# A ring of six weight blocks refilled one block at a time, and the heads' outputs transposed one step later, in a two-layer encoder trunk

## The chip, the cores and the metric

The kernel runs on one core of one Trainium2 chip. The time is the device time of one execution in microseconds (us). Before the change three runs gave 1183.42, 1184.66 and 1185.49 us, so the median is 1184.66 us. One further execution was taken with the hardware profiler, and every row of the profile below comes from that one.

## The reference

The kernel computes two layers over a sequence of 512 tokens of width 1024. Layer 0 mixes tokens by differential attention with six heads, and layer 1 by chunked gated linear attention (GLA). Each layer runs, beside its mixer, an attention of four heads into 256 memory tokens, sends all heads' outputs through one output projection, and ends with a gated MLP of inner width 2816 with a causal convolution. The part that the change touches most is the differential attention:

```python
lam = exp(sum(lv[0]*lv[1])) - exp(sum(lv[2]*lv[3])) + lam_init
logits = einsum('bhmqd,bhmkd->bhmqk', qb, k) + bias[rel]
p = softmax(where(visible, logits, -inf))
w = p[:, :, 0] - lam * p[:, :, 1]
o = einsum('bhqk,bhkv->bhqv', w, v)
o = rms_norm(o, out_norm_g) * (1.0 - lam_init)
```

Everything is float32. All weight products keep near float32 precision: each operand is split into a rounded high part and a low rest, and a product is the sum of three matmuls (high by high, high by low, low by high).

## The kernel before

**Weights.** Every weight matrix is cut into blocks of up to 128 x 1024 values, which lie in the order of their use in one packed input, wpack. A block is loaded by SyncE (SP) into one of three `raw` buffers (`load_raw`). ScalarE (ACT) then casts it to its high part `whi` (L203), and VectorE (DVE) subtracts to get the low part `wlo` (L206). whi and wlo each have a ring of five buffers (`WB = 5`), so the cast of a block waits for the last matmul that reads the block five places earlier. Blocks are grouped in pieces: a piece holds the weights of one gemm or one part of a projection, and has up to four blocks. `weights(key)` is called by the first unit of a gemm, and emits the loads, casts and subtractions of all blocks up to the end of the piece after it, in one go.

**Order on the engines.** TensorE (PE) runs its instructions in the order in which the program emits them. On the other engines the tile framework's scheduler orders the instructions that the program emits, with their waits. ACT and DVE each carry out their list in its order: an instruction that waits holds up all that stand behind it. Where the text speaks of the order after the change, it means the list of instructions that the changed program hands to an engine, which is known without a run.

**Fillers.** Projections that aren't urgent stand in a queue of units (`Filler`), each one pass of two k-tiles (six matmuls of 128 x 512). `F.fill(us)` takes units from the queue for about that many microseconds, so that PE has work while ACT and DVE work on the softmax.

**Layer 0.** A loop over steps t from 0 to 20 is written out as a software pipeline. A head has three steps. In step t the program does, in this order: `logits(t)` (matmuls L622 into banks `lg`, then DVE L627 for bias and minimum, and ACT L630 for exp), `values(t-2)` (L660 into a bank `sm`; at each third step the head's norm: squares on ACT L666, then the normed output `o` on DVE L670), `F.fill`, `turn(t-1)` (four transposes L172 into a bank `tp`, copied to SBUF by ACT L648), memory-attention work (`ma`), `F.fill` again, at t = 5, 6, 11, 12 `prepare` of a later head (transposes of `qs` and `ks`, copied with a gain by ACT L589 to qT and kT), and, at each third step from t = 5, `finish(t//3 - 1)`: four transposes of a head's `o` into a `tp` bank, then the split into xsh (ACT L240) and xsl (DVE L241), which the output projection reads much later. At t = 4 and 10 `norms` does the query and key norms of the next pair of heads (squares on ACT L310). There are two `tp` banks used in turn by all transposes, so a group of transposes waits until the group two before it has been copied out. The second memory projection of layer 0, kv of layer 1's memory, is evacuated by ACT L473 and L474.

**The rest.** The GLA layer, the output projections and the MLPs stream their weights through the same ring, with matmuls at L257 to L259 (weights moving) and L274 to L276 (weights stationary). The constants `C` (identity, masks, two unused triangles, ones) are loaded in the first microseconds, with the gate weights `gw` that the GLA layer uses.

Of the kernel before, what the change touches and what calls it, by code (L numbers as in the profile page):

```python
# [11 lines left out]
F32 = mybir.dt.float32  # L12
F32R = mybir.dt.float32r
I32 = mybir.dt.int32
# [10 lines left out]
MEM = 256  # L25
# [4 lines left out]
WTILE = 1024  # L30
HALVES = (6, 5)
XS = 36
WB = 5
STEPS, FILL = (11, 18), (3.7, 1.64, 1.5)

TOGETHER = ((2, 0), (1,), (3,))
# [95 lines left out]
def trunk(ctx, tc, head_d, x_t, mem_t, wpack, cols_a_d, cols_d, conv_d, gate_d, rel_bias, diff_lambda, consts, onehot, out):  # L132
# [26 lines left out]
    def blk(b, w=128):  # L159
        return slice(w * b, w * b + w)  # L160


    C = perm.tile([128, 768], F32, name="C")
    ident, U, BEU = C[:, 0:128], C[:, 128:256], C[:, 256:384]
    MP, MF = C[:, 384:512].bitcast(I32), C[:, 512:640].bitcast(I32)
    ones = C[:, 640:768]
    eps = perm.tile([128, 1], F32, name="eps")
    V.memset(eps, EPS)

# [38 lines left out]
    def raw_tile():  # L208
        return wp.tile([128, WTILE], F32, name="raw", tag="raw", bufs=3)

    def load_raw(raw, n):
        nc.sync.dma_start(raw[:, :n], wpack[at[0], :, :n])
        at[0] += 1
        return raw

    def make_piece(raws=None, between=None):
        parts = []
        for i, (_, _, kk, _, w) in enumerate(blocks[len(made)]):
            n = len(kk)
            raw = load_raw(raw_tile(), n * w) if raws is None else raws[i]  # L220
            hi, lo = (wp.tile([128, WTILE], F32R, name=t, tag=t, bufs=WB) for t in ("whi", "wlo"))
            if between is not None and i == 3:
                between()
            split_weights(slice(0, n * w), raw, hi, lo, len(made) == 2)
            parts += [(hi[:, blk(j, w)], lo[:, blk(j, w)]) for j in range(n)]
        made.append(parts)

    used = [0]

    def weights(key):  # L230
        i = used[0]
        assert plan[i][0] == key, (plan[i][0], key)
        while len(made) < min(i + 2, len(plan)):
            make_piece()
        used[0] += 1
        parts, made[i] = made[i], None
        return parts

    def split(hi, lo, src, gain):
        A.activation(hi, src, AF.Copy, scale=gain)  # L240
# [5 lines left out]
    def gemm(sh, sl, nb, key, w, evac, hook=None):  # L246
        got, open_ = [], {}

        def unit(b, k0, k1):
            if not got:  # L250
                got.extend(weights(key))
            if k0 == 0:
                open_[b] = bank("mm")[:, :w]
            p = open_[b]
            for k in range(k0, k1):
                hi, lo = got[k]
                mm(p, sh[k][:, blk(b)], hi, start=k == 0, stop=False)  # L257
                mm(p, sh[k][:, blk(b)], lo, start=False, stop=False)  # L258
                mm(p, sl[k][:, blk(b)], hi, start=False, stop=k == KT - 1)  # L259
            if k1 == KT:  # L260
                if hook is not None and b == 0:
                    hook()
                evac(b, open_.pop(b))
        for b in range(nb):
            for k in range(0, KT, 2):
                F.add(6 * w / 2370.0, lambda b=b, k=k: unit(b, k, k + 2))
# [16 lines left out]
    cols_a = perm.tile([128, 32], F32, name="cols_a")  # L283
    cols = perm.tile([128, 26], F32, name="cols")
    cv = [perm.tile([128, 4, NJ], F32, name=f"cv{l}") for l in range(2)]
    gw = perm.tile([96, 384], F32, name="gw")
    nlam = perm.tile([128, 1], F32, name="nlam")
    kmT = [perm.tile([128, 2, MEM], F32, name=f"kmT{l}") for l in range(2)]
    vm = [perm.tile([128, 2, MEM], F32, name=f"vm{l}") for l in range(2)]
    r_x = perm.tile([128, 3, 4], F32, name="r_x")  # L290
    r_mem = perm.tile([128, 2], F32, name="r_mem")

# [30 lines left out]
            V.tensor_copy(bs[c.start // 512], p[:6, :n])  # L323

    def lam(lv, lp):
        l2 = small("l2")[:, :2]
        lv4 = lv.rearrange("p (a c b) -> p a c b", a=2, c=2)
        V.tensor_mul(lp, lv4[:, :, 0], lv4[:, :, 1])
        V.reduce_sum(l2, lp, axis=AX.X)
        A.activation(l2, l2, AF.Exp)  # L330
        V.scalar_tensor_tensor(nlam, l2[:, 1:2], -LAM_INIT, l2[:, 0:1], op0=ALU.add, op1=ALU.subtract)
# [29 lines left out]
    with tc.tile_pool(name="ini", bufs=1) as ip, tc.manual_schedule(engines={E.Activation, E.DVE, E.Pool, E.SP}):  # L361
# [21 lines left out]
            load(raws[k // 2][:, blk(k % 2, S)], wpack[k // 2, :, blk(k % 2, S)])  # L383
        load(cols_a, cols_a_d)
        at[0] = 4
        load(C[:, 640:768], consts[:, 640:768])
        load(rb, rel_bias)
        load(oh, onehot)
        second = [load_raw(raw_tile(), WTILE) for _ in range(3)]
# [1 line left out]
        load(lv, diff_lambda[0].rearrange("a b -> (a b)").partition_broadcast(128))  # L391
        parts, acc, split_w = [], [None], [None]
        made.append(parts)

        def operands(k):
            if k % 2 == 0:
# [17 lines left out]
        for k in range(KT):  # L414
            if k + 1 < KT:
                operands(k + 1)
            if k == 0:
                second.append(load_raw(raws[0], WTILE))
            if k == 4:
                bias_rows(rb, oh, bs)  # L420
            if k == KT - 2:
                make_piece(second, lambda: token_rsqrt("lg", acc[0], NB, r_x[:, 0]))
                weights(("qk", 0))
                small_vectors()
                for c in range(2):
                    load(bias_d[:, 512 * c:min(512 * c + 512, 640)], bs[c])
            hi, lo = parts[k]
            terms = (xh[k], hi), (xh[k], lo), (xl[k], hi)
            full, left, right = slice(0, S), blk(0, S // 2), blk(1, S // 2)
            todo = [(b, i, full) for b in range(NB) for i in range(3)]  # L430
            if k == 0:
                todo = [(0, 0, left), (1, 0, left), (0, 0, right), (1, 0, right)] + sorted(
                    [u for u in todo if u[:2] not in ((0, 0), (1, 0))], key=lambda u: u[1])
            for b, i, t in todo:
                xp, w = terms[i]
                mm(first[b][:, t], xp[:, blk(b)], w[:, t], start=k == 0 and i == 0 and t is not right,
                   stop=k == KT - 1 and i == 2)

    load(C[:, 0:640], consts[:, 0:640])
    for i in range(4):  # L440
        load(memT[i], mem_t[i])
    for l in range(2):
        load(cv[l].rearrange("p a b -> p (a b)"), conv_d[l])
    G.memset(gw, 0.0)
    for b in range(3):
        load(gw[32 * b:32 * b + 17], gate_d)

    mem_acc = [None]

# [104 lines left out]
    def diff_layer(pool, mix, acc):  # L554
        r = r_x[:, 0]
        qm = pool.tile([128, NB, MEM], F32, name="qm", bufs=1)

        v0 = pool.tile([128, NB, 256], F32, name="v0", bufs=1)
        v12 = pool.tile([128, NB, 512], F32, name="v12", bufs=1)
        vs = [v0, v12[:, :, 0:256], v12[:, :, 256:512]]  # L560
# [135 lines left out]
        for t in range(21):  # L696
            if t == 0:
                project_qk(1)
                ops0, keys0 = mem_kv(0)
                gemm(xh, xl, NB, ("v", 1), 512, lambda b, p: A.activation(  # L700
                    v12[:, b], p, AF.Copy, scale=r[:, b:b + 1]))
                F.mark("v1")
                project_qk(2)
            if t == 2:
                ops0()
                ma.norm()
            if t == 10:
                ops1, keys1 = mem_kv(1)
                ops1()
            if t == 16:  # L710
                keys1()
            if t == 12:
                load_x(x_t)
                out_proj(0, mix, 0, None)
            if t == 18:
                rest = out_proj(0, mix, 1, acc, 5)
            f = FILL[bisect(STEPS, t)]
            m = t - M0
            if t < 18:
                logits(t)  # L720
            if 0 <= t - 2 < 18:
                values(t - 2)
            if t == 6:
                keys0("tp")
            F.fill(f)
            if t in (4, 10):
                norms((t + 2) // 6, 0)
                norms((t + 2) // 6, 1)
            if 0 <= t - 1 < 18:
                turn(t - 1)  # L730
            if 1 <= m < 5:
                ma.turn(2 * m - 2)
            if m in (3, 5):
                ma.values(m // 2 - 1)
            if 0 <= m < 4:
                ma.logits(m)
            if t == 20:
                F.flush()
            F.fill(f)
            if 1 <= m < 5:  # L740
                ma.turn(2 * m - 1)
            if t == 3:
                ma.queries()
            if t in (5, 6, 11, 12):
                prepare(2 * ((t + 1) // 6) + (t + 1) % 6)
            if t % 3 == 2 and t >= 5:
                finish(t // 3 - 1)
        rest()
        F.flush()

# [1 line left out]
    def gla_layer(pool, mix, acc):  # L752
# [6 lines left out]
        gl = pool.tile([128, NB, 16], F32, name="gl", bufs=1)  # L759
        gl3, gw3 = split_tiles()  # L760
        gl3, gw3 = gl3[:96], gw3[:96, :384]
        rq, rh = small("rq"), small("rh")

        def scales():
            token_rsqrt("sm", acc[0], NB, r_x[:, 2], True)
# [39 lines left out]

        G.memset(gl3.bitcast(F32), 1.0)
        G.memset(gl3[32:64].bitcast(F32), 0.0)
        A.copy(gw3, gw)
        V.tensor_sub(gw3[64:96], gw[64:96], gw3[64:96].bitcast(F32))
        F.fill(1.0)  # L810
# [313 lines left out]
def _constants():  # L1124
# [2 lines left out]
    i = np.arange(128)  # L1127
    same = (i[:, None] // 64) == (i[None, :] // 64)
    le = i[:, None] <= i[None, :]
    c = np.zeros((128, 768), np.float32)  # L1130
    c[:, 0:128] = np.eye(128)
    c[:, 128:256] = same & le
    c[:, 256:384] = same & ~le
    c[:, 384:512] = same & le
    c[:, 512:640] = same & ~le
    c[:, 640:768] = 1.0

    rel = np.arange(640) - 511
    n = np.abs(rel)
# [57 lines left out]
```

## Time and profile before

| what | value |
|---|---|
| median of three runs | 1184.66 us |
| the profiled execution, its own time | 1182.33 us |
| span of its instructions | 1180.5 us |
| so around the span | 1.8 us |
| PE | busy 99% of the span |
| PE weight loads | busy 82% |
| DVE | busy 64% |
| ACT | busy 46% |
| DMA | 117.81 MB at a mean of 100 GB/s |
| granted PE clock | 1.00 |

How to read it: the profile's groups name a line, an engine, an operation and the tile that is written and read; the value in brackets behind a timeline row is the time for which the engine stood idle just before it, and the instruction that ended that wait. Matmuls overlap: the 128 x 512 ones last 0.39 us each but start 0.23 us apart, so PE is called busy where one ends after the next has begun, and a wait shorter than the overlap isn't seen as idle time. The profiled execution is 2.33 us below the median of the three runs.

### The profile page before, as it was taken

Reading aid. Unit: us, or ns where it says so; the run is one execution under the profiler, and the core shown is the slowest. Engines: PE = TensorE matmul, PEld = TensorE weight load, DVE = VectorE, ACT = ScalarE, POOL = GpSimd, SP = SyncE. Lnnn points to the kernel's source line nnn. Section 1 sums busy time; section 2 is a strip of 40 time slices with the busy share of each in tenths; the row PEclk is TensorE's granted clock in tenths of the full one; section 3 lists DMA queues with packets and bytes.
Section 4 is the critical chain, followed back from the end, with each engine's and each line's share of the span. In section 5 each row is a group of like instructions: output and inputs, shape, how many; then the busy total and the mean of one; then the engine's idle time right before and its main releaser. Section 6 shows DMA issues by size and latency. Waiting matters only on the chain.

```text
span 1180.5 us, 14752 instructions
## 1 busy us (share of the span) xinstructions
PE 1169.2 (99%) x5658; PEld 965.8 (82%) x5658; DVE 757.1 (64%) x1252; ACT 546.2 (46%) x952; POOL 4.6 (0%) x25
## 2 busy tenths in 40 slices
PE   9999998999999999999999999999999999999998
PEld 7887886888888888888887788987888888888887
DVE  7567677587767335777557656768776743476741
ACT  6676676565434213444437535436443422343420
POOL 0000000000000000000000000000000000000000
PEclk9999999999999999999999999999999999999999
DMA  8323214132323232223341221333232233232231
GB/s 295 125 88 97 81 53 145 45 125 91 123 72 107 90 107 91 105 72 107 123 147 54 73 72 59 121 96 118 72 121 93 82 115 107 72 125 72 89 117 44
DMA packets 39556, 117.81 MB, mean 100 GB/s; under 512 B 4703, under 2 KB 7064, under 8 KB 39486
## 3 DMA queue, kind: packets, MB, share of 16 engines
q1 hardware_dynamic: 39054, 116.48, 29.3%
q8 instruction: 44, 0.72, 0.2%
q10 hardware_dynamic: 432, 0.39, 0.1%
q14 instruction: 26, 0.21, 0.1%
HBM read 112.65 MB, written 4.21 MB: 99 GB/s over the span
## 4 chain that ended last, share of the span: by engine, by line
PE 93%; DVE 3%; ACT 2%; issue 1%; POOL 0%; DVEq 0%; ACTq 0%; POOLq 0%
PE ps_mm L275 9%; PE ps_mm L276 9%; PE ps_mm L274 9%; PE ps_sm L274 7%; PE ps_sm L275 7%; PE ps_sm L276 7%; PE ps_mm L257 5%; PE ps_mm L259 5%; PE ps_mm L258 5%; PE ps_tp L275 3%; PE ps_tp L274 3%; PE ps_tp L276 3%; PE ps_lg L275 3%; PE ps_lg L276 3%; PE ps_lg L274 3%; PE ps_tp L172 2%
## 5 line engine op out<-in xcount | busy, mean ns | idle before, releaser
L203 ACT CAST whi<-raw 128x1024 fp32r<-128x1024 f32 (+4 forms) x212 | 208.5, 986 | 258.8 <-PE ps_tp L275 130.7
L206 DVE TENSOR_TENSOR wlo<-raw,whi 128x1024 fp32r<-128x1024 f32 (+4 forms) x212 | 241.2, 1140 | 107.0 <-ACT whi L203 106.0
L274 PE MATMUL ps_mm<-xsh,whi 128*128 128x512 f32 x438 | 173.0, 395 | 0.0
L275 PE MATMUL ps_mm<-xsl,whi 128*128 128x512 f32 x438 | 170.6, 389 | 0.2 <-DVE xsl L241 0.2
L276 PE MATMUL ps_mm<-xsh,wlo 128*128 128x512 f32 x438 | 170.6, 390 | 0.0
L274 PE MATMUL ps_sm<-xsh,whi 128*128 128x512 f32 x378 | 147.1, 389 | 0.0
L276 PE MATMUL ps_sm<-xsh,wlo 128*128 128x512 f32 x378 | 147.1, 389 | 0.0
L275 PE MATMUL ps_sm<-xsl,whi 128*128 128x512 f32 x378 | 147.0, 389 | 0.0
L257 PE MATMUL ps_mm<-whi,xsh 128*128 128x512 f32 (+2 forms) x352 | 136.1, 387 | 0.1
L259 PE MATMUL ps_mm<-whi,xsl 128*128 128x512 f32 (+2 forms) x352 | 131.1, 372 | 0.4 <-DVE xsl L241 0.4
L258 PE MATMUL ps_mm<-wlo,xsh 128*128 128x512 f32 (+2 forms) x352 | 130.7, 371 | 0.0
L1052 ACT ACTIVATE cvo<-u,cv 128x512 f32<-128x512 f32 x88 | 71.4, 813 | 121.4 <-DVE u L1050 121.4
L275 PEld LDWEIGHTS ps_mm<-xsl,whi 128*128 128x128 f32 x438 | 82.3, 188 | 17.7 <-DVE xsl L241 0.6
L276 PEld LDWEIGHTS ps_mm<-xsh,wlo 128*128 128x128 f32 x438 | 82.2, 188 | 17.2
L274 PEld LDWEIGHTS ps_mm<-xsh,whi 128*128 128x128 f32 x438 | 82.3, 188 | 16.9 <-issue 0.5
L1053 DVE SCALAR_TENSOR_TENSOR cvo<-u,cv,cvo 128x512 f32<-128x512 f32 x88 | 65.9, 749 | 38.7 <-ACT cvo L1052 38.7
L276 PEld LDWEIGHTS ps_sm<-xsh,wlo 128*128 128x128 f32 x378 | 70.9, 188 | 14.8
L275 PEld LDWEIGHTS ps_sm<-xsl,whi 128*128 128x128 f32 x378 | 70.9, 188 | 14.7
L274 PEld LDWEIGHTS ps_sm<-xsh,whi 128*128 128x128 f32 x378 | 71.0, 188 | 14.7
L257 PEld LDWEIGHTS ps_mm<-whi,xsh 128*128 128x128 f32 x352 | 66.2, 188 | 13.7 <-issue 3.3
L259 PEld LDWEIGHTS ps_mm<-whi,xsl 128*128 128x128 f32 x352 | 66.1, 188 | 12.5 <-DVE xsl L241 0.6
L258 PEld LDWEIGHTS ps_mm<-wlo,xsh 128*128 128x128 f32 x352 | 66.3, 188 | 10.0
(273 smaller groups left out, 1744.5 us busy)
## 6 DMA issues: line engine op xcount, KB each, us to landing
raw<-in_wpack_dram SPq DMA_DIRECT2D x178, 512.0 KB, 3.5
xt<-in_x_t_dram SPq DMA_DIRECT2D x15, 256.0 KB, 5.5
raw<-in_wpack_dram SPq DMA_DIRECT2D x15, 256.0 KB, 2.7
raw<-in_wpack_dram SPq DMA_DIRECT2D x8, 384.0 KB, 3.2
xres<-xt SPq DMA_DIRECT2D x8, 256.0 KB, 2.0
xt<-xres SPq DMA_DIRECT2D x8, 256.0 KB, 3.4
out_dram<-xt SPq DMA_DIRECT2D x7, 256.0 KB, 2.0
bt<-bias_d SPq DMA_DIRECT2D x6, 256.0 KB, 4.4
```

What stands on the lines that cost most here:

```text
L172: nc.tensor.transpose(dst, src, ident[:n, :n])
L203: ins = A.copy(hi[:, c], raw[:, c])
L206: V.tensor_sub(lo[:, c], raw[:, c], hi[:, c].bitcast(F32))
L257: mm(p, sh[k][:, blk(b)], hi, start=k == 0, stop=False)
L258: mm(p, sh[k][:, blk(b)], lo, start=False, stop=False)
L259: mm(p, sl[k][:, blk(b)], hi, start=False, stop=k == KT - 1)
L274: mm(p, hi[:, blk(n)], bh, start=i == first, stop=False)
L275: mm(p, hi[:, blk(n)], bl, start=False, stop=False)
L276: mm(p, lo[:, blk(n)], bh, start=False, stop=i == last)
L1052: A.activation(c, u[:, 2:], AF.Identity, scale=cv[l][:, 2, j:j + 1], bias=cv[l][:, 3, j:j + 1])
L1053: V.scalar_tensor_tensor(c, u[:, 1:S + 1], cv[l][:, 1, j:j + 1], c, op0=ALU.mult, op1=ALU.add)
```

## The change

1. The ring of whi and wlo gets six buffers in place of five.
2. Within a gemm blocks are no longer made a piece at a time. When a gemm starts, `weights(key, True)` makes blocks up to six from the gemm's first. Then, in the last pass over the tokens, `freed` makes one further block right behind the matmuls that read a block for the last time, so that its cast goes into the buffer that they free. Raw loads run up to three blocks ahead (`ahead`). The output projections and the MLPs go on making whole pieces, one piece ahead.
3. `finish(h)` moves from the end of step 3h + 5 to step 3h + 6, behind `logits` and `values` and ahead of the first `F.fill`, for h = 0 to 4. `finish(5)` stays at the end of step 20.
4. Room is made in SBUF: the two triangles leave the constants (768 columns become 512; the second load of them shrinks from 640 columns to 384), the gate weights are loaded by the GLA layer into a working tile just before they are used, kmT and vm of layer 0 move into that layer's pool, and three small tiles get fewer buffers.

What is computed stays the same, and each engine keeps about the same number of instructions: PE's list has the same 4873 rows, in which only the four transposes of five `finish` calls stand elsewhere; the casts are 212 before and after.

```diff
-WB = 5
+WB = 6
...
-    def make_piece(raws=None, between=None):
-        parts = []
-        for i, (_, _, kk, _, w) in enumerate(blocks[len(made)]):
-            n = len(kk)
-            raw = load_raw(raw_tile(), n * w) if raws is None else raws[i]
...
+    def ahead():
+        while len(raw_q) < 3 and done[0] + len(raw_q) < len(order):
+            _, n, w = order[done[0] + len(raw_q)]
+            raw_q.append(load_raw(raw_tile(), n * w))
+
+    def make_block(raws=None):
+        i, n, w = order[done[0]]
+        if raws is None:
+            ahead()
+            raw = raw_q.popleft()
...
+        hi, lo = (wp.tile([128, WTILE], F32R, name=t, tag=t, bufs=WB) for t in ("whi", "wlo"))
+        split_weights(slice(0, n * w), raw, hi, lo, i == 2)
...
-    def weights(key):
+    def weights(key, by_block=False):
         i = used[0]
...
-        while len(made) < min(i + 2, len(plan)):
-            make_piece()
+        limit = first_of[i] + WB if by_block else first_of[min(i + 2, len(plan))]
+        while done[0] < min(max(limit, first_of[i + 1]), len(order)):
+            make_block()
...
+    def freed(i, k):
+        if k in [sum(len(b[2]) for b in blocks[i][:j + 1]) - 1 for j in range(len(blocks[i]))] and done[0] < len(order):
+            make_block()
...
                 mm(p, sl[k][:, blk(b)], hi, start=False, stop=k == KT - 1)
+                if b == nb - 1:
+                    freed(piece, k)
...
             if 0 <= t - 2 < 18:
                 values(t - 2)
+            if t % 3 == 0 and t >= 6:
+                finish(t // 3 - 2)
             if t == 6:
                 keys0("tp")
...
-            if t % 3 == 2 and t >= 5:
-                finish(t // 3 - 1)
+            if t == 20:
+                finish(5)
...
+        gw = xtile()[:96, :384]
+        G.memset(gw, 0.0)
+        for b in range(3):
+            load(gw[32 * b:32 * b + 17], gate_d)
         A.copy(gw3, gw)
```

More of the change, by code (lines that the diff above doesn't have):

```diff
@@ L160, in blk @@
         return slice(w * b, w * b + w)
[L163 to L166, printed above, removed]
+    C = perm.tile([128, 512], F32, name="C")
+    ident = C[:, 0:128]
+    MP, MF = C[:, 128:256].bitcast(I32), C[:, 256:384].bitcast(I32)
+    ones = C[:, 384:512]
     eps = perm.tile([128, 1], F32, name="eps")
@@ L214, in load_raw @@
         return raw
-    def make_piece(raws=None, between=None):
-        parts = []
-        for i, (_, _, kk, _, w) in enumerate(blocks[len(made)]):
-            n = len(kk)
-            raw = load_raw(raw_tile(), n * w) if raws is None else raws[i]
[L221 to L226, printed above, removed]
+    order = [(i, len(b[2]), b[4]) for i, piece in enumerate(blocks) for b in piece]
+    first_of = [sum(len(q) for q in blocks[:i]) for i in range(len(blocks) + 1)]
+    done, raw_q = [0], deque()
+    def ahead():
[7 more added lines that the diff above has]
+            raw = raw_q.popleft()
+        else:
+            raw = raws.pop(0)
+        done[0] += 1
+        while len(made) <= i:
+            made.append([])
+        hi, lo = (wp.tile([128, WTILE], F32R, name=t, tag=t, bufs=WB) for t in ("whi", "wlo"))
+        split_weights(slice(0, n * w), raw, hi, lo, i == 2)
+        made[i] += [(hi[:, blk(j, w)], lo[:, blk(j, w)]) for j in range(n)]
+        if raws is None:
+            ahead()
     used = [0]
-    def weights(key):
+    def weights(key, by_block=False):
         i = used[0]
         assert plan[i][0] == key, (plan[i][0], key)
-        while len(made) < min(i + 2, len(plan)):
-            make_piece()
+        limit = first_of[i] + WB if by_block else first_of[min(i + 2, len(plan))]
+        while done[0] < min(max(limit, first_of[i + 1]), len(order)):
+            make_block()
         used[0] += 1
@@ L247, in gemm @@
         got, open_ = [], {}
+        piece = [q[0] for q in plan].index(key)
         def unit(b, k0, k1):
             if not got:
-                got.extend(weights(key))
+                got.extend(weights(key, True))
             if k0 == 0:
@@ L285, in trunk @@
     cv = [perm.tile([128, 4, NJ], F32, name=f"cv{l}") for l in range(2)]
-    gw = perm.tile([96, 384], F32, name="gw")
     nlam = perm.tile([128, 1], F32, name="nlam")
-    kmT = [perm.tile([128, 2, MEM], F32, name=f"kmT{l}") for l in range(2)]
-    vm = [perm.tile([128, 2, MEM], F32, name=f"vm{l}") for l in range(2)]
+    kmT = [None, perm.tile([128, 2, MEM], F32, name="kmT1")]
+    vm = [None, perm.tile([128, 2, MEM], F32, name="vm1")]
     r_x = perm.tile([128, 3, 4], F32, name="r_x")
@@ L325, in lam @@
     def lam(lv, lp):
-        l2 = small("l2")[:, :2]
+        l2 = small("l2", 1)[:, :2]
         lv4 = lv.rearrange("p (a c b) -> p a c b", a=2, c=2)
@@ L385, in trunk @@
         at[0] = 4
-        load(C[:, 640:768], consts[:, 640:768])
+        load(C[:, 384:512], consts[:, 384:512])
         load(rb, rel_bias)
@@ L393, in trunk @@
         made.append(parts)
+        done[0] = 4
         def operands(k):
@@ L421, in trunk @@
             if k == KT - 2:
-                make_piece(second, lambda: token_rsqrt("lg", acc[0], NB, r_x[:, 0]))
-                weights(("qk", 0))
+                for j in range(4):
+                    if j == 3:
+                        token_rsqrt("lg", acc[0], NB, r_x[:, 0])
+                    make_block(second)
+                weights(("qk", 0), True)
                 small_vectors()
@@ L437, in trunk @@
                    stop=k == KT - 1 and i == 2)
-    load(C[:, 0:640], consts[:, 0:640])
+    load(C[:, 0:384], consts[:, 0:384])
     for i in range(4):
@@ L443, in trunk @@
         load(cv[l].rearrange("p a b -> p (a b)"), conv_d[l])
-    G.memset(gw, 0.0)
-    for b in range(3):
-        load(gw[32 * b:32 * b + 17], gate_d)
     mem_acc = [None]
@@ L556, in diff_layer @@
         qm = pool.tile([128, NB, MEM], F32, name="qm", bufs=1)
+        kmT[0] = pool.tile([128, 2, MEM], F32, name="kmT0", bufs=1)
+        vm[0] = pool.tile([128, 2, MEM], F32, name="vm0", bufs=1)
         v0 = pool.tile([128, NB, 256], F32, name="v0", bufs=1)
@@ L761, in gla_layer @@
         gl3, gw3 = gl3[:96], gw3[:96, :384]
-        rq, rh = small("rq"), small("rh")
+        rq, rh = small("rq", 2), small("rh", 1)
         def scales():
@@ L1129, in _constants @@
     le = i[:, None] <= i[None, :]
-    c = np.zeros((128, 768), np.float32)
+    c = np.zeros((128, 512), np.float32)
     c[:, 0:128] = np.eye(128)
@@ L1133, in _constants @@
     c[:, 256:384] = same & ~le
-    c[:, 384:512] = same & le
-    c[:, 512:640] = same & ~le
-    c[:, 640:768] = 1.0
+    c[:, 384:512] = 1.0
     rel = np.arange(640) - 511
```

## The prediction, made before the changed kernel was run

> **What bounds the kernel now.** The first view is the page's list of busy times, with the shares of the chain of work that ended last.
>
> ```profile
> PE 1169.2 (99%) x5658; PEld 965.8 (82%) x5658; DVE 757.1 (64%) x1252; ACT 546.2 (46%) x952; POOL 4.6 (0%) x25
> PE 93%; DVE 3%; ACT 2%; issue 1%; POOL 0%; DVEq 0%; ACTq 0%; POOLq 0%
> ```
>
> PE is busy for 1169.2 of 1180.5 us and carries 93% of the chain. The change gives PE the same instructions, so its work can't shrink; only its waits can, and they are 1180.5 - 1169.2 = 11.3 us. The second view, the busy time in stretches of 30 us, says where they lie (the second number is PE's busy time); the third, the list of PE's waits (us in total, times, longest), says for whom.
>
> ```profile
> 180.00:210.00 30.00, 25.92 (x164) 20.98 (x163) 20.63 (x64) 20.20 (x56) 0.00 (x0) 1.00 0.37 132
> 1170.00:1180.50 10.50, 7.14 (x32) 5.59 (x30) 1.44 (x3) 0.00 (x0) 0.00 (x0) 1.00 0.14 50
> ```
>
> ```profile
> PE ps_tp L172 <- ACT xt L648: 2.9, 1, 2.9
> PE ps_tp L172 <- ACT qT L589: 1.5, 2, 1.2
> PE ps_tp L370 <- POOL idle L367: 1.3, 1, 1.3
> PE ps_mm L259 <- DVE xsl L241: 0.4, 1, 0.4
> ...
> PE ps_tp L172 <- DVE xt L524: 0.2, 1, 0.2
> ```
>
> One stretch of layer 0 loses 30 - 25.92 = 4.1 us, and the end (the last add and store) 3.4 us. In the list, 1.3 us is the start. No wait names whi or wlo: PE never waits for weights. What the change can win is thus 11.3 - 3.4 - 1.3 = 6.6 us, of which 4.4 are the two waits on top. The other waits of the list are 0.2 to 0.4 us each, 6.6 - 4.4 = 2.2 us together.
>
> The fourth view is the timeline of ACT in that stretch, step t = 12, and the fifth that of PE.
>
> ```profile
> 180.41 0.82 ACT L203 CAST whi<-raw 128x768 fp32r<-128x768 f32 x1
> 181.71 0.69 ACT L589 ACTIVATE kT<-ps_tp,cols 128x512 f32<-128x512 f32 x1
> 185.67 0.83 ACT L203 CAST whi<-raw 128x768 fp32r<-128x768 f32 x1 [2.41 <-PE ps_mm L259]
> 187.05 0.84 ACT L203 CAST whi<-raw 128x768 fp32r<-128x768 f32 x1 [0.55 <-PE ps_mm L259]
> 188.87 0.47 ACT L473 ACTIVATE xt<-ps_mm,r_mem 128x256 f32<-128x256 f32 x1 [0.98 <-PE ps_mm L259]
> 189.60 0.61 ACT L630 ACTIVATE xt<-xt,nmd 128x384 f32<-128x384 f32 x1
> 191.56 0.57 ACT L648 COPY xt<-ps_tp 128x512 f32<-128x512 f32 x1
> ```
>
> ```profile
> 179.68 0.60 PE L172 MATMUL ps_tp<-C,qs 128*128 128x128 f32 x4
> 180.11 0.60 PE L172 MATMUL ps_tp<-C,ks 128*128 128x128 f32 x4
> 181.87 0.66 PE L172 MATMUL ps_tp<-C,o 128*128 128x128 f32 x4 [1.16 <-ACT qT L589]
> 182.46 1.14 PE L622 MATMUL ps_lg<-kT,qT 64*128 64x192 f32 x12
> ...
> 186.85 0.60 PE L172 MATMUL ps_tp<-C,xt 128*128 128x128 f32 x4
> ...
> 188.67 0.60 PE L172 MATMUL ps_tp<-C,qs 128*128 128x128 f32 x4
> 192.19 0.66 PE L172 MATMUL ps_tp<-C,ks 128*128 128x128 f32 x4 [2.92 <-ACT xt L648]
> ```
>
> The ks transposes at 192.19 want the bank that turn(11) filled at 186.85. Its copy stands last in ACT's list, behind two casts and an evacuation that waited 2.41, 0.55 and 0.98 us for PE to free their buffers or end their sum, and behind the exps of logits(12), whose matmuls were through at 183.60. ACT stood still with work at hand, and PE paid 2.92 us.
>
> **The change part by part.**
>
> *The ring and the release by block.* In the changed program's list for ACT the order at t = 12 is: cast, qT, kT, the four exps, xsh of finish(2), a cast of 768, one of 1024, the copy of turn(11), a cast of 256, the evacuation. With a sixth buffer each of these casts takes the buffer for which the cast before it waited, so the 768 is free to go at 185.67 and the 1024 at 187.05. By the rows: the exps last 191.56 - 189.60 = 1.96 us and can start when DVE has the first of the logits, about 184, so they end near 186.0; xsh, of kT's form and so 0.69, makes 186.7, the 768 cast 0.83 makes 187.5, the 1024 cast (1.0, row below) 188.5, and the copy's 0.57 makes 189.1. PE wants the bank after the qs transposes, 188.67 + 0.43 (179.68 to 180.11 is the pitch of four) = 189.10, and 0.45 later by the next item. So I take the whole 2.92 away: **-2.9 us**. Bounds: -3.1 (with the overlap that hides the first part of a wait) and 0 (the copy is held as before, a rival).
>
> The Trainium skill's page "Perfetto Trace Analysis", section "Optimization Strategy", speaks against this: it takes the same gap repeating on the engine that should be saturated as the sign of too few buffers. This trace does not show that sign on PE, whose longest wait comes once. By that rule the deeper ring would bring nothing here and the sum below would lose its -2.9; by the rows the 2.41 and 0.55 us that ACT waited for buffers are links of this one wait, and I go by them.
>
> *finish behind the logits.* The next view is the same place at t = 6, on PE and then on ACT.
>
> ```profile
> 104.75 0.66 PE L172 MATMUL ps_tp<-C,o 128*128 128x128 f32 x4 [0.34 <-ACT qT L589]
> 105.34 0.92 PE L622 MATMUL ps_lg<-kT,qT 64*128 64x192 f32 x8
> ```
>
> ```profile
> 104.59 0.68 ACT L589 ACTIVATE kT<-ps_tp,cols 128x512 f32<-128x512 f32 x1
> ```
>
> The logits begin at 105.34, just behind the end of kT at 104.59 + 0.68 = 105.27; at t = 12 at 182.46, behind 181.71 + 0.69 = 182.40. So the four transposes of `o`, which waited for qT's bank, stood inside the wait for kT. Moved behind the logits they leave that wait as it is, now before L622, and add their own length after it: 0.43 (pitch above) to 0.59 us (104.75 to 105.34), I take **+0.45 each, +0.9 together**. The 1.5 us in the list doesn't go; it is renamed. Below nothing I don't go, since kT stands behind the same work on ACT. At t = 9, 15 and 18 the list shows no wait at finish, the move crosses no other user of the tp banks, and the fill behind it covers the split on ACT and DVE: nothing, with 0.2 us (its smallest rows) either way.
>
> *Casts ahead of another copy.* At t = 10, in ACT's order:
>
> ```profile
> 164.94 2.00 ACT L203 CAST whi<-raw 128x1024 fp32r<-128x1024 f32 x2
> ...
> 171.29 0.60 ACT L648 COPY xt<-ps_tp 128x512 f32<-128x512 f32 x1
> 171.76 0.87 ACT L203 CAST whi<-raw 128x768 fp32r<-128x768 f32 x1
> 172.49 0.35 ACT L193 ACTIVATE rs_y<-ss,eps 128x16 f32<-128x16 f32 x1
> 172.87 0.22 ACT L194 ACTIVATE rs_y<-rs_y 128x16 f32<-128x16 f32 x1
> ```
>
> ```profile
> 171.97 0.63 PE L172 MATMUL ps_tp<-C,xt 128*128 128x128 f32 x4
> ```
>
> The copy of turn(9) ends at 171.89, and the transposes that want its bank start 0.08 later: no slack. In the new list two casts of 1024 and two of 768 stand ahead of it, in place of three of 1024 (two of them in the row at 164.94), and so does a norm's Ln and exp. A 1024 cast takes half of 2.00 us, a 768 one 0.73 (171.76 to 172.49), Ln and exp 0.35 + 0.22. That is 2 x 0.73 - 1.00 + 0.57 = 1.0 us more, so the copy ends near 172.9 and PE starts about 0.95 late. Part of it is swallowed at t = 12, where PE waits 1.16 us for ACT anyway; how much depends on whether kT's work on ACT starts later too. Bounds 0 and +1.0, I take the middle, **+0.5**.
>
> *The other short waits* (2.2 us) lie at PE's waits for DVE and ACT in the memory attention and the GLA layer, where each cast now stands a place or so elsewhere in ACT's list: I take 0, with -2.2 (all go) and +2.2 (each doubles).
>
> *Loads and room.* SP issues three gate loads late, behind one raw load and a POOL memset; constants shrink.
>
> ```profile
> raw<-in_wpack_dram SPq DMA_DIRECT2D x178, 512.0 KB, 3.5
> 615.51 0.50 ACT L808 CAST xsl<-gw 96x384 fp32r<-96x384 f32 x1
> 628.52 0.60 PE L172 MATMUL ps_tp<-C,gl 128*16 128x128 f32 x4
> ```
>
> The cast of gw ran at 615.51, and PE turns gl, the other operand of its product, only at 628.52. A landing of 3.5 us fits between. So nothing, and if that cover were gone up to 3.5 us. Raw loads run up to three ahead as there are three raw buffers; with no PE wait on weights they cost nothing.
>
> **Sum.** -2.9 + 0.9 + 0.5 = -1.5 us: the profiled execution goes from 1182.33 (span 1180.5 and 1.8 around it) to about 1180.8. That execution lies 2.3 below the median of the runs, 1184.66, so the median goes to **1183.2 us**.
>
> **Rivals.**
> 1. *All short waits go as well*, and the copy at t = 10 is swallowed: -2.9 + 0.9 - 2.2 = -4.2, so 1180.5. For it: waits behind casts have one cause, and a sixth buffer eases it everywhere. Against it: most of the short waits name DVE, not a cast.
> 2. *The wait at 192.19 stays*, the change not doing what it says: a cast still holds the copy until the sum at 188.87 ends. Then +0.9 + 0.5 = +1.4, so 1186.1. For it: the list still has two casts ahead of the copy. Against it: by the rows above their buffers are free 1.8 us before that. The Trainium skill's rule on repeated gaps, in the section cited above, would come out here.
> 3. *Slower: casts given out sooner overtake copies.* Each block is now emitted where its buffer comes free, so in ACT's list it stands ahead of the copies that free tp banks. It strikes at t = 10 and at t = 4, which has the same norms; the price is one cast, about 0.95 us, for each that stands ahead or waits. It decides when such copies cost more than 2.0 us in all, the sum's 0.5 among them (three casts); with three at each of two places it is 6 x 0.95 = 5.7, and -2.9 + 0.9 + 5.7 = +3.7, so 1188.4. For it: the 0.08 us of slack at 171.97. Against it: no other copy shows so little.
>
> **How the numbers follow.** Forecast 0.47, rival 1 0.22, rival 2 0.13, rival 3 0.16, anything else 0.02. The range runs from rival 1's time, less 1.0 us, half the 2.07 between the lowest and highest run before, to just short of rival 3's: 1179.5 to 1188.0, with about 0.2 left out. This kernel's measurement tells some 0.2%, 2.37 us, from no change: faster than 1182.3 is most of rival 1 (0.20), the lower third of the forecast (0.15) and 0.01 of the rest, 0.36; slower than 1187.0 most of rival 3 (0.14), 0.03 of rival 2 and 0.01, 0.18; between them 0.46.
>
> **What would show it.** In the changed profile the stretch 180 to 210 should have PE busy for over 28 us, and the list of PE's waits no 2.9 us by a copy of turn; the waits for kT should stand at the logits, about 1.8 us in two; near 172 transposes should wait about 1 us for a copy of turn. Wrong would be the ring's term if the wait at 192 is over 1 us; the third item if nothing waits near 172; and the whole if waits over 1 us turn up in steps that had none.

## The result, and the profile after

The changed kernel takes 1180.98 us, median of nine runs (1180.14 to 1181.93). The kernel before, run beside it, takes 1183.72 us, median of nine (1182.33 to 1185.49). The ratio is 0.9976, 95% interval 0.9966 to 0.9986: 2.7 us less, a little more than the 0.2% named in the prediction. The profiled execution went from 1182.33 to 1180.98 us and its span from 1180.5 to 1179.2 us, only 1.3 us less. So half of what the medians show isn't in the two profiles; where it went is taken up at the end of the experiments.

The page of the changed kernel, and its stretches with PE's busy time as the second number:

```profile
PE 1168.3 (99%) x5658; PEld 966.6 (82%) x5658; DVE 757.1 (64%) x1252; ACT 547.1 (46%) x952; POOL 4.6 (0%) x25
```

```profile
150.00:180.00 30.00, 28.63 (x197) 23.12 (x197) 23.07 (x58) 21.65 (x61) 0.00 (x0) 1.00 0.18 58
180.00:210.00 30.00, 28.79 (x190) 23.44 (x185) 22.85 (x70) 20.60 (x59) 0.14 (x1) 1.00 0.41 128
```

The stretch 180 to 210 lost 4.1 us before and loses 1.2 now; the stretch 150 to 180 lost nothing and loses 1.4 now. The list of PE's waits (us in total, times, longest):

```profile
PE ps_lg L648 <- ACT kT L615: 2.1, 2, 1.2
PE ps_tp L393 <- POOL idle L390: 1.3, 1, 1.3
PE ps_mm L299 <- DVE xsl L261: 0.8, 1, 0.8
PE ps_tp L172 <- DVE xsl L261: 0.7, 1, 0.7
PE ps_tp L172 <- ACT xt L674: 0.7, 1, 0.7
PE ps_tp L172 <- DVE xt L548: 0.7, 2, 0.4
...
```

The 2.9 us by a copy of turn are gone. The wait for qT is now a wait for kT at the logits, and three waits of 0.7 to 0.8 us are new or longer. PE's timeline has them in place (lines are those of the changed kernel: L648 is the logits' matmul, L674 the copy of turn, L261 the low part of a split):

```profile
105.55 1.14 PE L648 MATMUL ps_lg<-kT,qT 64*128 64x192 f32 x12 [0.92 <-ACT kT L615]
...
107.61 0.60 PE L172 MATMUL ps_tp<-C,xt 128*128 128x128 f32 x4
...
151.75 0.66 PE L172 MATMUL ps_tp<-C,xt 128*128 128x128 f32 x4 [0.70 <-DVE xsl L261]
152.34 0.44 PE L571 MATMUL ps_sm<-xt,vm 128*64 128x128 f32 x4
...
174.37 0.66 PE L172 MATMUL ps_tp<-C,xt 128*128 128x128 f32 x4 [0.67 <-ACT xt L674]
...
184.36 1.14 PE L648 MATMUL ps_lg<-kT,qT 64*128 64x192 f32 x12 [1.22 <-ACT kT L615]
...
189.18 0.60 PE L172 MATMUL ps_tp<-C,xt 128*128 128x128 f32 x4
...
191.44 0.60 PE L172 MATMUL ps_tp<-C,ks 128*128 128x128 f32 x4
```

Since PE's list is the same but for five groups, the start of one and the same group in both profiles gives a ledger. Two rows of the kernel before that weren't shown yet:

```profile
106.96 0.60 PE L172 MATMUL ps_tp<-C,xt 128*128 128x128 f32 x4
...
150.79 0.44 PE L547 MATMUL ps_sm<-xt,vm 128*64 128x128 f32 x4
```

| group | before | after | later by | so this step |
|---|---|---|---|---|
| logits(6) | 105.34 | 105.55 | +0.21 | +0.21, ahead of any move |
| keys, behind finish(0) | 106.96 | 107.61 | +0.65 | +0.44 |
| values of the memory attention, t = 9 | 150.79 | 152.34 | +1.55 | +0.90 |
| transposes behind turn(9)'s copy | 171.97 | 174.37 | +2.40 | +0.85 |
| logits(12) | 182.46 | 184.36 | +1.90 | -0.50 |
| turn(11), behind finish(2) | 186.85 | 189.18 | +2.33 | +0.43 |
| ks of the next head | 192.19 | 191.44 | -0.75 | -3.08 |
| end of the span | 1180.5 | 1179.2 | -1.3 | -0.55 in all later steps |

### The profile page after: what moved, and what is told of

It reads as the page before. It is cut to its first block, busy times and chain, and to the rows that moved or that the text cites. A ratio compares the mean times of both kernels' runs of the same rounds, so it can differ in the third digit from the quotient of the medians.

```text
span 1179.2 us, 14803 instructions
## 1 busy us (share of the span) xinstructions
PE 1168.3 (99%) x5658; PEld 966.6 (82%) x5658; DVE 757.1 (64%) x1252; ACT 547.1 (46%) x952; POOL 4.6 (0%) x25
## 4 chain that ended last, share of the span: by engine, by line
PE 95%; ACT 2%; DVE 2%; issue 1%; POOL 0%; DVEq 0%; ACTq 0%; POOLq 0%
PE ps_mm L299 9%; PE ps_mm L298 9%; PE ps_mm L300 9%; PE ps_sm L300 7%; PE ps_sm L299 7%; PE ps_sm L298 7%; PE ps_mm L279 5%; PE ps_mm L281 5%; PE ps_mm L280 5%; PE ps_lg L298 3%; PE ps_lg L299 3%; PE ps_lg L300 3%; PE ps_tp L298 3%; PE ps_tp L299 3%; PE ps_tp L300 3%; PE ps_tp L172 2%
```

## The experiments

Two theories were tried against each other. **A** is the forecast's: the deeper ring lets ACT's casts go sooner, and that takes the wait at 192 away. **B**: the move of finish does it, since the four exps of logits(12) then stand ahead of the waiting casts in ACT's list. The letters C and F name rivals to B in single runs. A further question, with theories D and E, is the spread of the runs before. Each diff is against the kernel named ahead of it.

### The ring alone

This starts from the changed kernel.

```diff
-            if t % 3 == 0 and t >= 6:
-                finish(t // 3 - 2)
...
-            if t == 20:
-                finish(5)
+            if t % 3 == 2 and t >= 5:
+                finish(t // 3 - 1)
```

> The changed kernel with finish put back to the end of step 3h + 5: a ring of six, given out by block, and nothing moved on TensorE. Theory A (the forecast's: the deeper ring lets the casts go sooner, and that takes the 2.9 us wait at 192 away): the wait stays away, and without the moved transposes (0.9 us) the time is about 1180.0 us. Rival B (the wait went because finish moved: in this kernel's list for ScalarE the copy of turn(11) again stands behind three casts, the evacuation and the four exps, as before the change): the wait is back with some 3 us, and the time is about 1180.98 + 3.1 - 0.9 - 0.9 (the new wait near 152, if finish causes it) = 1182.3 us.

Measured: 1184.46 us against 1183.55 before, ratio 1.0003 (0.9994 to 1.0012). The ring of six with release by block, without the move, gains nothing. The first wait of PE's list, and ACT's timeline at t = 12:

```profile
PE ps_tp L172 <- ACT xt L674: 3.9, 2, 3.2
```

```profile
182.70 0.69 ACT L260 ACTIVATE xsh<-ps_tp,cols 128x512 fp32r<-128x512 f32 x1 [0.17 <-PE ps_tp L172]
185.80 0.84 ACT L203 CAST whi<-raw 128x768 fp32r<-128x768 f32 x1 [2.42 <-PE ps_mm L281]
187.17 1.05 ACT L203 CAST whi<-raw 128x1024 fp32r<-128x1024 f32 x1 [0.54 <-PE ps_mm L281]
189.00 0.41 ACT L203 CAST whi<-raw 128x256 fp32r<-128x256 f32 x1 [0.77 <-PE ps_mm L281]
...
190.03 0.61 ACT L656 ACTIVATE xt<-xt,nmd 128x384 f32<-128x384 f32 x1
...
192.00 0.57 ACT L674 COPY xt<-ps_tp 128x512 f32<-128x512 f32 x1
```

The waits of 2.42 and 0.54 us for buffers are those of before. The casts that meet them are of 768 and 1024, where before they were of 768 and 768: ACT is further on in the order of the blocks and meets the same waits. The exps and the copy stand behind them, and PE waits 3.2 us. A is refuted. B's time of 1182.3 us was missed by 2.2: the one execution at a granted clock of 1.000 took 1182.94 us, and the ten others, with 0.997 to 0.999, took 1183.28 to 1185.58. That clock is taken up in the last experiment.

### The move alone

This starts from the kernel before.

```diff
+            if t % 3 == 0 and t >= 6:
+                finish(t // 3 - 2)
...
-            if t % 3 == 2 and t >= 5:
-                finish(t // 3 - 1)
+            if t == 20:
+                finish(5)
```

> The kernel before with finish alone moved behind the logits; the ring stays at five and whole pieces are made. Theory A: the wait at 192 stays, the moved transposes add 0.9 us, so about 1184.6 us. Rival B: the four exps stand ahead of the two casts in ScalarE's list and the copy of turn(11) right behind these, so the wait goes with the old ring too: 1183.7 - 3.1 + 0.9 = about 1181.5 us, up to 1182.4 if the new wait near 152 belongs to finish as well. No wait near 172, since the casts at t = 10 stand as before.

Measured: 1181.09 us, ratio 0.9975 (0.9965 to 0.9986), as the whole change. ACT's timeline of this kernel, with the ring of five:

```profile
186.20 0.62 ACT L630 ACTIVATE xt<-xt,nmd 128x384 f32<-128x384 f32 x1 [1.92 <-DVE nmd L627]
...
188.19 0.67 ACT L240 ACTIVATE xsh<-ps_tp,cols 128x512 fp32r<-128x512 f32 x1
188.76 1.56 ACT L203 CAST whi<-raw 128x768 fp32r<-128x768 f32 x2
190.21 0.58 ACT L648 COPY xt<-ps_tp 128x512 f32<-128x512 f32 x1
```

The exps run in the time in which ACT used to stand still, and when ACT comes to the casts their buffers are free: no wait is shown at them. This fits B and not A.

### The ring of six with whole pieces

This starts from the changed kernel.

```diff
-                got.extend(weights(key, True))
+                got.extend(weights(key))
...
-                if b == nb - 1:
-                    freed(piece, k)
...
-                weights(("qk", 0), True)
+                weights(("qk", 0))
```

> The changed kernel (ring of six, finish moved) with the release by block taken out: each weights call makes whole pieces up to the next one, as before the change. Both theories: no wait at 192. What the release by block costs at t = 10 goes, since here the copy of turn(9) again stands ahead of the 768 casts and the norm's Ln: the wait of 0.7 us near 174 goes and the time is 0.4 to 0.9 us below the changed kernel, about 1180.3 us. If release by block helps elsewhere, it is not below, 1181 to 1182 us.

Measured: 1180.57 us, ratio 0.9974 (0.9961 to 0.9987). The wait near 174 is gone, as both theories had it; the difference of 0.4 us from the changed kernel is small beside the intervals of the two ratios, so only the wait's going is shown, not a gain.

### Release by block with a ring of five

This starts from the changed kernel.

```diff
-WB = 6
+WB = 5
```

> The changed kernel with the ring at five again; release by block and the moved finish stay. Theory A in its strict form (the sixth buffer is what matters): the casts wait one block longer, the copy of turn(11) is late again and the wait at 192 comes back with 1 to 3 us, 1182 to 1184 us. Rival B: no wait over 0.5 us at 192; at t = 10 a 1024 cast stands in place of a 768 one, so the copy of turn(9) comes 0.3 us later: about 1181.2 us.

Measured: 1181.41 us, ratio 0.9975 (0.9965 to 0.9985). Nothing waits at 192; the wait for turn(9)'s copy is 0.8 in place of 0.7 us. A in its strict form falls. The wait for xsl near 797 is 0.2 us here, as before the change, and 0.8 in the three kernels above that have six buffers: there a cast of 1024 stands ahead of the split that PE waits for, in place of one of 256. The sixth buffer has a price of its own, some 0.6 us at this place.

### finish(2) alone, and the other four alone

```diff
+            if t % 3 == 0 and t >= 6 and t // 3 - 2 in (2,):
+                finish(t // 3 - 2)
...
-            if t % 3 == 2 and t >= 5:
+            if t % 3 == 2 and t >= 5 and t // 3 - 1 not in (2,):
                 finish(t // 3 - 1)
```

The second kernel has (0, 1, 3, 4) in place of (2,). Both start from the kernel before.

> The kernel before with one of the five moves alone: finish(2), the one at t = 12, goes behind the logits; ring of five, whole pieces. Theory B (the move at t = 12 puts the exps ahead of the waiting casts in ScalarE's list, and nothing else of the change pays): the wait at 192 goes, and with it the drop of the granted clock that some executions of the kernel before have behind it (0.997 over the whole run against 1.000); the two moves that cost (0.44 us at t = 6, 0.86 at t = 9) are left out, so about 1181.1 - 1.3 = 1179.8 us. Rival C (the ring or the other moves have a share in it): 1180.5 us or more.

> The kernel before with the other four moves (finish(0), (1), (3) and (4)), finish(2) left in its place. Theory B: the wait of 2.9 us at 192 stays, and the moves cost 0.44 + 0.86: about 1183.6 + 1.3 = 1184.9 us. Rival C: some of the wait goes, 1183.6 us or less.

Measured: finish(2) alone 1179.43 us, ratio 0.9966 (0.9953 to 0.9978); the other four 1185.45 us, ratio 1.0016 (1.0008 to 1.0025). So one move of five has the whole gain and the rest cost, as B had it, the second by 0.5 us more than expected. The list of PE's waits of the kernel with the other four:

```profile
PE ps_tp L172 <- ACT xt L648: 2.9, 1, 2.9
...
PE ps_tp L172 <- DVE xsl L241: 0.7, 1, 0.7
```

The wait of 2.9 us is there, and the wait of 0.7 us at t = 9 comes without any change to the ring: it belongs to the move of finish(1).

### The ring of six with whole pieces and finish(2) alone

This is the kernel with a ring of six and whole pieces, in which finish(2) alone is moved.

> The ring of six with whole pieces and finish(2) alone moved. Theory B with a ring that is worth nothing by itself: as finish(2) alone, near 1179.8 us, within 0.5 us of it to either side (it won 1.0 us at short waits and lost 0.8 us near 798 where it was run with all moves). Rival C, the ring helps once the costly moves are gone: 1179.3 us or less.

Measured: 1179.83 us, ratio 0.9968 (0.9956 to 0.998). Within 0.5 us of finish(2) with the ring of five: no gain from the ring is shown. Its profiled span was the shorter of the two, 1177.6 against 1178.1 us, and its three executions at a granted clock of 1.000 have a median of 1179.21, against 1179.38 of the five of the other; a share below what these runs resolve stays open.

### The transposes left, the split written later

This starts from the kernel before.

```diff
-            mh, ml = split_tiles()
-            split(mh, ml, p, c_do)
-            mix[h] = (mh, ml)
-
+            def rest():
+                mh, ml = split_tiles()
+                split(mh, ml, p, c_do)
+                mix[h] = (mh, ml)
+            if h == 2:
+                late.append(rest)
+            else:
+                rest()
+
+        late = []
...
+            if t == 12:
+                late.pop()()
             if t == 6:
```

> The kernel before with TensorE's order left as it was: the transposes of finish(2) stay at the end of step 11, and only the split of their result on ScalarE and VectorE is written behind logits(12) and values(10). Ring of five, whole pieces. In ScalarE's list the four exps now stand ahead of xsh and of the casts, the copy of turn(11) behind one 768 cast. Theory B (the order on ScalarE's list is what took the wait at 192 away, not the place of the transposes and not the ring): the wait goes, the transposes hide in the wait for kT as before, and the time is finish(2) alone less 0.44 us: about 1179.0 us. Rival F (the place of the transposes on TensorE matters by itself): the wait stays above 1 us, 1181 us or more.

Measured: 1179.12 us, ratio 0.9959 (0.9946 to 0.9971), the fastest of all kernels here. PE's timeline of it:

```profile
181.92 0.66 PE L172 MATMUL ps_tp<-C,o 128*128 128x128 f32 x4 [1.17 <-ACT qT L589]
182.51 1.14 PE L622 MATMUL ps_lg<-kT,qT 64*128 64x192 f32 x12
...
188.72 0.60 PE L172 MATMUL ps_tp<-C,qs 128*128 128x128 f32 x4
189.15 0.60 PE L172 MATMUL ps_tp<-C,ks 128*128 128x128 f32 x4
```

Up to 188.72 it is the kernel before, within 0.05 us; then the ks transposes follow without a wait. PE's order is the old one and so is the ring; only the order on ACT and on DVE is new. ACT's list now has the exps, a cast and the copy of turn(11) in this order:

```profile
184.38 0.62 ACT L630 ACTIVATE xt<-xt,nmd 128x384 f32<-128x384 f32 x1 [1.93 <-DVE nmd L627]
...
186.94 0.82 ACT L203 CAST whi<-raw 128x768 fp32r<-128x768 f32 x1
187.66 0.58 ACT L648 COPY xt<-ps_tp 128x512 f32<-128x512 f32 x1
```

DVE's list changed with it. The exps need the result of L627, DVE's step for bias and minimum. In the profile of the kernel before it stood behind two subtractions, which themselves waited for ACT's waiting casts:

```profile
186.53 0.96 DVE L206 TENSOR_TENSOR wlo<-raw,whi 128x768 fp32r<-128x768 f32 x1 [2.49 <-ACT whi L203]
187.92 0.96 DVE L206 TENSOR_TENSOR wlo<-raw,whi 128x768 fp32r<-128x768 f32 x1 [0.43 <-ACT whi L203]
188.79 0.55 DVE L627 CUSTOM_DVE_ANT_0 xt<-ps_lg,bt 128x384 f32<-128x384 f32 x1
```

With the split written late it starts five us earlier, as soon as the logits are through:

```profile
183.78 0.56 DVE L627 CUSTOM_DVE_ANT_0 xt<-ps_lg,bt 128x384 f32<-128x384 f32 x1 [1.51 <-PE ps_lg L622]
```

B is shown, with the addition that the order changed on both engines; no run changes it on one alone. Rival F falls. Why the scheduler lists the work in the other order when this one split is written later, no run shows. Beside it on the same chip the changed kernel ran once more:

> The changed kernel itself, on the same chip as the split written late, to compare the two. All theories: 1181.0 us as before, 1.5 to 2 us above the split written late if theory B holds; its waits near 152, 174 and 797 as in its first profile.

Measured: 1181.22 us, ratio 0.9975 (0.9965 to 0.9985), 2.1 us above the split written late. That exceeds the 1.5 to 2 us expected by a little.

### One more copy ahead of the wait

This starts from the kernel before.

```diff
+            if t == 11:
+                idle2 = xtile()
+                A.copy(idle2, live[t])
+                A.copy(idle2, live[t])
             A.copy(wT[:, :n], pt[:, :n])
```

The scheduler put one of the two copies ahead of turn(11)'s.

> The kernel before with one more copy of 128 x 512 on ScalarE, of no use to the result, ahead of the copy of turn(11): about 0.6 us, so the wait at 192 grows from 2.9 to about 3.5 us. Theory D (the spread of the runs before comes from the TensorE clock, which drops for a few us behind a wait of about that length, in some executions): now nearly every execution has the drop, the granted clock over the run is 0.999 or less in all of them, and the median rises by 1 to 2 us, more than the 0.6 us that were added, to 1184.8 to 1185.8 us. Rival E (the spread has another cause): the median rises by 0.6 us to 1184.2 and the share of executions at 1.000 stays as it was.

Measured: 1184.30 us against 1183.68, ratio 1.0007 (0.9999 to 1.0016). The median rose by 0.6 us, as E said and D did not, though the interval of the ratio doesn't exclude that nothing changed. But the share of executions with a granted clock of 1.000 over the run fell from 6 of 22 to 0 of 12, as D said and E did not; twelve executions are few for that. In the 22 runs before, the time goes with that clock: 1182.14 to 1182.42 us at 1.000, 1183.23 to 1183.82 at 0.999, 1184.56 to 1185.69 at 0.997, 1186.43 at 0.996. The median lay among those with 0.999 with and without the extra copy, so D's step to a higher median was wrong. Its mechanism, a fall of the clock behind the wait, is in the profile. The stretches around the wait, in the profile of this kernel (PE's clock is the third number from the end):

```profile
189.00:192.00 3.00, 0.00 (x0) 0.00 (x0) 1.48 (x7) 3.00 (x12) 0.00 (x0) 1.00 0.96 362
192.00:194.00 2.00, 1.88 (x14) 1.50 (x15) 0.92 (x5) 2.00 (x5) 0.00 (x0) 0.80 0.04 14
194.00:196.00 2.00, 2.00 (x10) 1.90 (x9) 1.59 (x4) 2.00 (x8) 0.00 (x0) 0.50 0.00 0
196.00:198.00 2.00, 2.00 (x11) 1.58 (x10) 0.72 (x3) 1.81 (x10) 0.00 (x0) 0.84 0.23 66
```

Behind the wait, here 3.44 us, the clock falls to half and is full again some 4 us on. Two stretches of the kernel with the other four moves, whose wait was 2.92 us as in the profile before:

```profile
192.00:194.00 2.00, 0.88 (x6) 0.55 (x6) 1.27 (x4) 2.00 (x7) 0.00 (x0) 0.86 0.87 337
194.00:196.00 2.00, 2.00 (x12) 1.77 (x13) 0.83 (x5) 1.54 (x3) 0.00 (x0) 0.50 0.01 4
```

So a wait of the old length can be followed by it too. The ring alone, with a wait of 3.22 us, shows the same:

```profile
194.00:196.00 2.00, 2.00 (x9) 2.00 (x10) 1.15 (x6) 1.09 (x5) 0.00 (x0) 0.50 0.07 29
```

The profile of the kernel before shows 1.00 throughout, as it is one of the executions that escaped. The mean clock over a run is a rough sign only. The changed kernel's profile has 0.999 as well, but there the fall lies behind PE's last matmul, where it costs PE nothing:

```profile
1176.00:1179.20 3.20, 0.00 (x0) 0.00 (x0) 0.60 (x2) 0.00 (x0) 0.00 (x0) 0.80 0.24 82
```

## Why the prediction came out as it did

**The time** was right: 1183.2 us forecast, 1180.98 measured, in the range, and faster. Of the 2.2 us between the two, 0.9 are the base: the later runs put the kernel before at 1183.72, where three runs had 1184.66. The other 1.3 us are about what the clock took from the median execution before: 1183.7 less the 1182.3 of the executions at full clock is 1.4 us. The sum was made from a profile at full clock and applied to a median that wasn't. That the gain between the medians holds this share is worked out from the clocks and times of the runs; the fall of the clock itself is in profiles of three other kernels, and none was taken of an execution of the kernel before that had it. Between the two profiles, which is what the sum was made for, -1.5 us were forecast and -1.3 measured. That they lie so close is luck in part: the terms below miss by +0.9 at t = 9 and by -0.55 at the short waits, and these and smaller misses nearly cancel.

**The wait at 192, -2.9**: it measured -3.08, but the step was put to the wrong part of the change. The prediction wrote it under "the ring and the release by block" and reasoned that "each of these casts takes the buffer for which the cast before it waited". The list it read, exps ahead of casts, was right; what had made that list was not asked. Its sign of being wrong, a wait of over 1 us at 192, could not tell the ring from the move, as the changed program had both. Its reading that ACT stood still "with work at hand" doesn't hold for the exps either: their input came from DVE only behind 188.79. The ring alone left the wait at 3.2 us, and the split of finish(2) written later, with the old ring, took it away. The Trainium skill, page "Perfetto Trace Analysis", section "Optimization Strategy", says of repeated gaps only that they can mean too few buffers. That without such gaps a deeper ring brings nothing was the prediction's own conclusion from it; the ring alone agrees with that conclusion, with a ratio of 1.0003.

**The moved transposes, +0.9**: +0.44 and +0.43 in the ledger; the wait for qT turned into one for kT, as forecast.

**The move at t = 9, taken as nothing**: +0.90. The claim that failed is that the fill behind it covers the split. The kernel with the other four moves has this wait with the old ring, so it belongs to the move. Behind logits(9) the split of finish(1) stands after four exps on ACT, its tp bank comes free late, and transposes two groups on wait 0.70 us for xsl. The list of waits before could not show it; the reader of that list would have had to follow the bank.

**The casts at t = 10, +0.5**: +0.85 where 0.95 was estimated, and 0.50 of it swallowed at t = 12, so +0.35. Right.

**The other short waits, 0 with 2.2 either way**: -0.55 in the profile, with the wait near 797 grown from 0.2 to 0.8 us inside it.

**Rivals**: of the first one's short waits, 2.2 us, a net 0.55 went by the ledger. The second one's mechanism, a copy still held by casts, is what the ring does alone; in the whole change it didn't occur. The third's, a late copy of turn, occurred once at the price of one cast and not at t = 4.

## What to carry to other kernels

When an engine that works through its list in order stands still at a wait, look at what stands behind that wait, in its list and in the list of the engine that feeds it, before adding buffers. Here writing one split a few lines later put other work ahead of the waits, and won 4.5 us (3.1 of them between the profiled spans) where a deeper ring won none. Try each part of a change alone; here one of five moves had all the gain. And before a median is compared with a profile, look whether that execution ran at the same granted clock as the others.

## What was not expected of the hardware

One wait of PE of 2.9 to 3.4 us, in a kernel otherwise dense with matmuls, was followed in profiles of three kernels by a granted clock of 0.50 for at least 2 us. With the extra copy, matmuls behind it then started 0.42 us apart (195.74 to 196.17 to 196.59) in place of 0.23, and about 1.6 us were lost beyond the wait: the ks transposes start at 192.12, before 192.19, but the matmul that starts at 195.10 before starts at 196.59. By the mean clock of the run, with a wait of 2.9 us 16 of 22 executions were below 1.000, with 3.4 us 12 of 12, and of the kernel with the split written late, whose longest wait is 1.3 us, none of 5. These counts are not of this wait alone. The changed kernel, whose longest wait is 1.3 us too, was below 1.000 in 7 of 18. The ring of six with finish(2) alone, whose longest is 1.8, took 1179.07 to 1179.38 us in three executions at 1.000 and 1180.28 to 1180.67 in three at 0.999. The ring of six with whole pieces, whose longest is 1.8 too, had one execution of 1183.80 us at 0.997. What slowed these is not on record. The Trainium skill, page "TensorE: Matmul & The Clock Gate", section "HAM oscillation", has PE fall to half clock at gaps above about 3.4 us; the half clock agrees with the 0.50 here, and the length is less in these runs: 2.92 and 3.22 us were followed by it.
